# Low parts of w8 formed by VectorE differences instead of adding transfers

## The chip, the cores and the metric

The kernel runs on one core of a Trainium2 chip. The metric is the device time of one launch in microseconds; the median over several runs is compared. Five engines work side by side, each taking its own instructions in order: TensorE (PE; its weight loads are listed apart as PEld), VectorE (DVE), ScalarE (ACT), GpSimd (POOL) and SyncE (SP), which here only issues transfers. They wait for one another by semaphores. Transfers run on 16 DMA engines.

## What is computed

Two transformer layers on a sequence of 512 tokens with 1024 features, in float32. The first layer mixes four kinds of heads and ends with a gated FFN. The second one modulates its norms by a vector c, runs a state-space mixer beside windowed attention, and ends with the FFN in which the change lies:

```python
mod = (c_act @ w_mod[l] + b_mod[l])[:, None, :]
sh1, sc1, g1, sh2, sc2, g2 = jnp.split(mod, N_MOD, axis=-1)
...
h2 = _rms(x, norm2_w[l]) * (1 + sc2) + sh2
x = x + g2 * _conv_ffn(h2, w_up[l], conv_w[l], conv_b[l], w_down[l])

def _conv_ffn(h, w_up, conv_w, conv_b, w_down):
    up = h @ w_up
    up = <causal depthwise conv of width 3 over the tokens> + conv_b
    val, gate = jnp.split(up, 2, axis=-1)
    return (jax.nn.silu(gate) * val) @ w_down
```

w_up is 1024 x 5632 here (w8 in the kernel) and w_down 2816 x 1024 (w9).

## The kernel before, in words

**Split products.** Every matrix product is made of three products in the format fp32r, of which a value keeps only the upper part: hi = fp32r(w), lo = w - hi, and likewise for the activations; hi*hi + hi*lo + lo*hi is summed in PSUM (`mm3`, L451, called by `proj_f`, L457, and `proj_group`, L463). So each weight must be turned into a hi tile (`whi`) and a lo tile (`wlo`) before TensorE can use it.

**Weight pieces.** All weights stand in one list, `queue`, in the order in which they are used, cut into pieces of at most 128 x 1072 values (`cut`, L326). A w8 piece is 128 columns of w_up over all 8 k-tiles (512 KB), one group of 24 matmuls over 512 tokens; a w9 piece is 4 k-tiles by 256 columns, also 24 matmuls (the first four are half as large). `_Lazy.load` (L367) issues the transfer into a `raw` tile (two buffers, SP's queue), has ScalarE round it into `whi` (five buffers), and forms `wlo` (five buffers) in one of two ways:

```python
act(v(hi)[:, a:b], v(raw)[:, a:b], AF.Copy)                               # L374
if self.name in DMA_LO:
    act(lo[:, :m], raw[:, :m], AF.Copy, scale=-1.0)                       # L377
    nc.gpsimd.dma_start(v(lo), self.src[...], accum_op=ALU.add)           # L378
else:
    V.tensor_tensor(v(lo)[:, a:b], v(raw)[:, a:b], v(hi...), op=ALU.subtract)   # L381
```

The first way writes the negated rounded value and has a transfer issued by GpSimd add the weight from memory to it a second time. The second way is one VectorE instruction, which holds the raw buffer until it is done. Before, w6, w7 and w8 go the first way, all others the second.

**The second FFN** (`ffn`, L1254, called at L1738) walks over six chunks of hidden features: `up` makes for each hidden tile two groups (value and gate), `down` multiplies the chunk before by w9. Its groups take their PSUM banks in turn from three pools, tr (2 banks), sc (2) and acc (3). `hidden2` (L1723) evacuates a pair: for each half ScalarE writes `cf` from PSUM (L1717) and VectorE adds two shifted rows to it (L1719, 511 and 510 columns wide); then Silu (L1726), a product (L1727) and the split into `hd` (L507, L508). `down2` (L1733) adds a w9 product to x.

**Modulation rows.** The last eight rows of the modulation (g2, `modG`) are computed in the head of this FFN: `modulation` (L1069) is a generator that is advanced twice after each group of the FFN; each row is two transfers of 256 KB into `wm` (three buffers, SP's queue) and two VectorE reductions with the vector `cb` (L1082). Each is held back until the split of the latest hidden tile has been issued.

**Before the FFN** stands the norm (`norm_tail`, L1291): the six last tiles of x are made in two halves of tokens, squared by ScalarE (L1340), summed by VectorE (L1342), and normalised (L512 to L521); `modulated` (L1358) makes h2 from them, `hm` and `hl` on VectorE, `hl` on ScalarE. The first three w8 pieces are loaded during this time; a limit on the list keeps the others back until h2 is complete, after which `go_on` (L390) loads the next one. The first three groups run k-tile by k-tile as h2 comes (`start_ffn2`, L1690).

The order of instructions on each engine is set by the scheduler of the language from its own estimates, except on TensorE where parts are held in the order written.

Of the kernel before, what the change touches and what calls it, by code (L numbers as in the profile page):

```python
# [46 lines left out]
NW = 16  # L47
NHL = 5
SUM_E = "vector"
DMA_LO = ("w6", "w7", "w8")  # L50
LAG = 4
NRAW = 2
NW2 = 19
# [179 lines left out]
def build(tc, I, out, PV, PVN, CS, CSN, CS1, CSN1):  # L233
# [105 lines left out]
    class _Lazy:  # L339
# [27 lines left out]
        def load(self):  # L367
# [5 lines left out]
            for a, b in self.halves():  # L373
                act(v(hi)[:, a:b], v(raw)[:, a:b], AF.Copy)  # L374
            if self.name in DMA_LO:
                k0, k1, c0, c1 = self.cut
# [1390 lines left out]
```

## Time and profile before

| | |
|---|---|
| median of three runs | 1287.53 us (1284.62 to 1288.72) |
| the profiled execution | 1290.43 us |
| its span, first to last instruction | 1288.6 us |
| TensorE busy | 1230.1 us, 95% |
| VectorE busy | 836.3 us, 65% |
| ScalarE busy | 553.8 us, 43% |
| GpSimd busy | 312.1 us, 24% |
| moved by DMA | 192.95 MB, of them 40.61 MB on GpSimd's queue |
| w8 and w9 stage (second FFN) | from 901.89 us to the end |

Times in the rows are microseconds from the start of the span. "Idle before" a group is the time that its engine stood just before its instructions, and the name behind the arrow is what ended that wait. A granted clock of 1.00 is 2.4 GHz of TensorE, 0.50 is 1.2 GHz.

### The profile page before, as it was taken

The numbers are of one execution on the slowest core, as the hardware profiler recorded it, in microseconds if no ns is written. First come the engines' busy times: TensorE is split into PE (matmuls) and PEld (weight loads), VectorE is DVE, ScalarE is ACT, GpSimd is POOL, SyncE is SP. The second block draws the span as 40 slices with busy tenths as digits, with TensorE's granted clock in tenths as the row PEclk, the third lists the DMA queues.
The fourth block names the chain that finished last, engine by engine and source line by source line (L and its number), as shares of the span: only waits on it lengthen the run. The fifth ranks groups of instructions, "written<-read, shape, count | busy, mean of one in ns | idle before, by whom it ended". The sixth has DMA issues, their size and how long they took to land.

```text
span 1288.6 us, 17279 instructions
## 1 busy us (share of the span) xinstructions
PE 1230.1 (95%) x6269; PEld 993.0 (77%) x6269; DVE 836.3 (65%) x1622; ACT 553.8 (43%) x918; POOL 312.1 (24%) x399
## 2 busy tenths in 40 slices
PE   7899999999999999999999978889899999999998
PEld 6788765667887878888889877668777788888886
DVE  7668868677977967676667488756547343434362
ACT  6334465454332323232325235765655544444430
POOL 1000004113409283755201331032121211111200
PEclk9999999999999999999999887989899999999999
DMA  6431111126356665666547865457799989796921
GB/s 223 156 112 49 51 33 50 50 61 191 115 162 202 218 200 181 188 194 198 176 144 248 246 150 129 122 129 129 140 209 194 211 168 161 148 177 141 186 82 66
DMA packets 211156, 192.95 MB, mean 150 GB/s; under 512 B 13056, under 2 KB 173712, under 8 KB 211072
## 3 DMA queue, kind: packets, MB, share of 16 engines
q1 hardware_dynamic: 154528, 146.96, 37.8%
q0 software_dynamic: 51456, 40.61, 19.8%
q10 hardware_dynamic: 5088, 4.29, 1.0%
q8 instruction: 50, 0.82, 0.3%
q14 instruction: 34, 0.28, 0.1%
HBM read 178.22 MB, written 15.43 MB: 150 GB/s over the span
## 4 chain that ended last, share of the span: by engine, by line
PE 76%; DVE 9%; issue 5%; DMA 5%; ACT 4%; POOL 1%; SPq 0%; POOLq 0%; DVEq 0%; ACTq 0%
PE acc L261 51%; PE sc L261 12%; PE tr L261 8%; DMA raw<-in_w_dram 3%; PE po L261 2%; DMA wlo<-in_w_dram 2%; DVE wlo L381 1%; PE tr L886 1%; ACT whi L374 1%; DVE z L1478 1%; DVE z L1467 1%; PE tr L1616 1%; DVE z L1466 1%; POOL keep L929 0%; POOL wlo L378 0%
## 5 line engine op out<-in xcount | busy, mean ns | idle before, releaser
L261 PE MATMUL acc<-hl,whi 128*128 128x512 f32 (+1 forms) x1624 | 483.6, 381 | 10.3 <-ACT whi L374 6.1
L374 ACT ACTIVATE whi<-raw 128x1024 fp32r<-128x1024 f32 (+2 forms) x188 | 194.3, 1035 | 392.7 <-PE acc L261 231.4
L261 PEld LDWEIGHTS acc<-hl,whi 128*128 128x128 f32 x1624 | 295.3, 189 | 77.4 <-issue 9.2
L261 PE MATMUL acc<-hl,wlo 128*128 128x512 f32 (+1 forms) x812 | 308.5, 380 | 0.3 <-DMA wlo<-in_w_dram 0.3
L381 DVE TENSOR_TENSOR wlo<-raw,whi 128x1024 fp32r<-128x1024 f32 (+2 forms) x134 | 174.9, 1307 | 67.7 <-ACT whi L374 64.7
L261 PEld LDWEIGHTS acc<-hl,wlo 128*128 128x128 f32 x812 | 153.1, 189 | 31.6 <-issue 3.1
L378 POOL DMA_DIRECT2D wlo<-in_w_dram x54 | 72.0, 1334 | 326.7 <-ACT wlo L377 225.7
L261 PE MATMUL acc<-hd,whi 128*128 128x512 f32 (+1 forms) x472 | 143.1, 386 | 2.1 <-DVE x L1348 2.1
L261 PE MATMUL acc<-whi,hl 128*128 128x256 f32 (+1 forms) x544 | 110.3, 294 | 3.3 <-ACT whi L374 1.7
L261 PEld LDWEIGHTS acc<-hd,whi 128*128 128x128 f32 x472 | 87.0, 188 | 21.6 <-issue 3.1
L261 PEld LDWEIGHTS acc<-whi,hl 128*128 128x128 f32 x544 | 90.0, 197 | 8.8 <-ACT tok L248 3.0
L261 PE MATMUL acc<-hd,wlo 128*128 128x512 f32 (+1 forms) x236 | 91.0, 386 | 0.0
L1082 DVE CUSTOM_DVE_ANT_0 wm<-wm,cb 128x512 f32<-128x512 f32 x96 | 78.0, 844 | 14.3 <-DMA wm<-in_wmod_dram 14.2
L261 PE MATMUL acc<-wlo,hl 128*128 128x256 f32 (+1 forms) x272 | 79.4, 292 | 0.7 <-DVE wlo L381 0.7
L261 PE MATMUL tr<-hl,whi 128*128 128x512 f32 (+1 forms) x240 | 75.2, 397 | 0.0
L261 PE MATMUL sc<-hl,whi 128*128 128x512 f32 x208 | 65.0, 393 | 0.0
L377 ACT ACTIVATE wlo<-raw 128x1024 fp32r<-128x1024 f32 x54 | 56.5, 1045 | 4.8 <-DMA raw<-in_w_dram 2.8
L261 PE MATMUL tr<-hl,wlo 128*128 128x512 f32 (+1 forms) x120 | 48.1, 400 | 8.9 <-DMA wlo<-in_w_dram 8.9
L261 PEld LDWEIGHTS acc<-wlo,hl 128*128 128x128 f32 x272 | 53.8, 198 | 2.5 <-DVE wlo L381 1.0
L929 POOL TENSOR_SCALAR_AFFINE_SELECT keep<-keep 128x128 f32<-128x128 f32 x16 | 9.3, 594 | 185.8 <-ACT keep L923 185.0
L261 PEld LDWEIGHTS tr<-hl,whi 128*128 128x128 f32 x240 | 46.3, 196 | 10.2
L261 PEld LDWEIGHTS acc<-hd,wlo 128*128 128x128 f32 x236 | 44.4, 188 | 9.4
(427 smaller groups left out, 1945.6 us busy)
## 6 DMA issues: line engine op xcount, KB each, us to landing
raw<-in_w_dram SPq DMA_DIRECT2D x176, 512.0 KB, 4.4
wlo<-in_w_dram POOLq DMA_DIRECT2D x54, 512.0 KB, 7.8
wm<-in_wmod_dram SPq DMA_DIRECT2D x96, 256.0 KB, 4.1
xk<-in_xT_dram SPq DMA_DIRECT2D x16, 256.0 KB, 4.6
raw<-in_w_dram SPq DMA_DIRECT2D x10, 256.0 KB, 4.0
d_g<-s5g POOLq DMA_DIRECT2D x4, 576.0 KB, 4.0
gt<-d_g SPq DMA_DIRECT2D x4, 576.0 KB, 6.1
w1c<-in_w1k_dram SPq DMA_DIRECT2D x8, 256.0 KB, 6.1
```

What stands on the lines that cost most here:

```text
L261: nc.tensor.matmul(o, lhsT=l, rhs=r, start=start, stop=stop, **k)
L374: act(v(hi)[:, a:b], v(raw)[:, a:b], AF.Copy)
L377: act(lo[:, :m], raw[:, :m], AF.Copy, scale=-1.0)
L378: nc.gpsimd.dma_start(v(lo), self.src[:, k0:k1, c0:c1], accum_op=ALU.add)
L381: V.tensor_tensor(v(lo)[:, a:b], v(raw)[:, a:b], v(hi.bitcast(F32))[:, a:b], op=ALU.subtract)
L886: nc.tensor.transpose(tp[:, q * P:(q + 1) * P], pr[hh][:, j * P:(j + 1) * P], ident)
L929: G.affine_select(g[:, d], g[:, d], fill=1.0, **past)
L1082: V.tensor_tensor_reduce(wm, wm, cb[:, n * 512:(n + 1) * 512], 1.0, 0.0, ALU.mult, ALU.add, mh[:, n, j:j + 1])
L1466: V.scalar_tensor_tensor(dst[re], src[im], sign, t[im], op0=ALU.mult, op1=ALU.mult)
L1467: V.scalar_tensor_tensor(dst[im], src[re], -sign, t[re], op0=ALU.mult, op1=ALU.mult)
L1478: V.tensor_tensor_scan(z2[:, c], mag8[:, q * 8 + g:q * 8 + g + 1].to_broadcast([P, 64]), z[:, c], 0.0, ALU.mult, ALU.add)
L1616: nc.tensor.transpose(tp[:, m * P:(m + 1) * P], probs[n][:, hh, (j - j0) * P:(j - j0 + 1) * P], ident)
```

## The change

One name is taken out of a tuple; nothing else differs between the two files.

```diff
@@ -47,7 +47,7 @@
 NW = 16
 NHL = 5
 SUM_E = "vector"
-DMA_LO = ("w6", "w7", "w8")
+DMA_LO = ("w6", "w7")
 LAG = 4
 NRAW = 2
 NW2 = 19
```

With it the 44 pieces of w8 take the second way in `load`: L377 and L378 are not issued for them, L381 is. w6 and w7 keep the first way. The description of the change also speaks of evenly spaced modulation rows; their code is the same in both files. The scheduler sets some instructions in another order. Three places show it; a row is line, operation, out<-in and shape, and x2 stands for two such rows.

VectorE between the norm and the first evacuations of the second FFN: `hl` is the low part of h2, `cf` the conv rows of the first two groups.

```order
 L1362 SCALAR_TENSOR_TENSOR hm<-x_7_8176,a_3143,r_8191 128x256
 L1367 SCALAR_TENSOR_TENSOR hl<-hm,modT,hl 128x256 x2
+L381 TENSOR_TENSOR wlo<-raw,whi 128x1024 x2
 L1719 SCALAR_TENSOR_TENSOR cf<-acc,pv,cf 128x511 x2
 L1719 SCALAR_TENSOR_TENSOR cf<-acc,pv,cf 128x510 x2
 L1719 SCALAR_TENSOR_TENSOR cf<-acc,pv,cf 128x511
+L381 TENSOR_TENSOR wlo<-raw,whi 128x1024
+L1727 TENSOR_TENSOR cf<-cf 128x512
 L1719 SCALAR_TENSOR_TENSOR cf<-acc,pv,cf 128x510
-L1727 TENSOR_TENSOR cf<-cf 128x512
 L1719 SCALAR_TENSOR_TENSOR cf<-tr,pv,cf 128x511
```

The differences of the fourth and fifth piece come right behind h2, that of the sixth between the conv rows of the first groups.

ScalarE at the same place:

```order
 L519 ACTIVATE rsq<-r_8191 128x256
 L1366 ACTIVATE hl<-hm,modT 128x256 x9
-L374 ACTIVATE whi<-raw 128x1024
-L377 ACTIVATE wlo<-raw 128x1024
-L374 ACTIVATE whi<-raw 128x1024
-L377 ACTIVATE wlo<-raw 128x1024
+L374 ACTIVATE whi<-raw 128x1024 x2
 L1074 ACT_TABLE_LOAD
 L1074 ACTIVATE cb<-cb 128x1024
 L1717 ACTIVATE cf<-acc,pv 128x512 x3
```

The negated copies of the fourth and fifth piece are gone from between the two roundings.

VectorE in the norm, where the second w8 piece is made ready (`xa` and `x` are the sums of a tile of x, `sqsum` the sum of squares):

```order
 L1679 SCALAR_TENSOR_TENSOR xa<-acc,gm,r_a 128x512
 L1680 TENSOR_TENSOR x_1_7983<-x_1_7983,xa 128x512
+L381 TENSOR_TENSOR wlo<-raw,whi 128x1024
 L1679 SCALAR_TENSOR_TENSOR xa<-acc,gm,r_a 128x256
+L1342 TENSOR_TENSOR sqsum<-sqsum,sq 128x512
 L1680 TENSOR_TENSOR x_2_8011<-x_2_8011,xa 128x256
-L1342 TENSOR_TENSOR sqsum<-sqsum,sq 128x512
 L1679 SCALAR_TENSOR_TENSOR xa<-acc,gm,r_a 128x256
```

A difference stands between the tiles 1 and 2 of x; another stands earlier, ahead of the root for r_a, and a third between the second halves of tiles 3 and 4, just ahead of the root of this norm. On TensorE only the small products of the norm move by two or three matmuls. On GpSimd the 44 issues of L378 are missing. On SP the loads of raw and of modulation rows change places a few times.

## Rows read from the trace of the kernel before

**Rows 1.** The page: busy us (share of the span) and instructions of each engine
```profile
PE 1230.1 (95%) x6269; PEld 993.0 (77%) x6269; DVE 836.3 (65%) x1622; ACT 553.8 (43%) x918; POOL 312.1 (24%) x399
```
**Rows 2.** Busy time by stage: stretch, length, PE PEld DVE ACT POOL, clock, DMA, GB/s
```profile
400.00:690.00 290.00, 289.81 (x1343) 236.09 (x1342) 204.95 (x302) 89.16 (x117) 138.77 (x211) 1.00 0.60 187
...
925.00:930.00 5.00, 2.94 (x7) 2.42 (x8) 1.38 (x3) 1.17 (x3) 1.44 (x1) 0.50 1.32 223
...
915.00:985.00 70.00, 61.02 (x269) 49.56 (x269) 34.05 (x69) 37.38 (x48) 12.94 (x9) 0.93 1.03 208
985.00:1240.00 255.00, 254.05 (x1098) 205.90 (x1096) 111.62 (x147) 119.94 (x143) 45.99 (x32) 1.00 0.88 166
```
**Rows 3.** TensorE's waits after 905 us: in total, times, longest
```profile
PE tr L261 <- DMA wlo<-in_w_dram: 8.9, 2, 6.4
PE sc L261 <- DMA wlo<-in_w_dram: 0.6, 1, 0.6
PE acc L261 <- DMA wlo<-in_w_dram: 0.3, 1, 0.3
```
**Rows 4.** TensorE in order of time: start, length, instruction [idle before <-releaser]
```profile
901.89 0.97 PE L261 MATMUL acc<-hl,whi 128*128 128x256 f32 x4 [2.75 <-ACT hl L1366]
...
920.00 0.63 PE L261 MATMUL tr<-hl,whi 128*128 128x512 f32 x2
927.06 0.77 PE L261 MATMUL tr<-hl,wlo 128*128 128x512 f32 x1 [6.43 <-DMA wlo<-in_w_dram]
...
934.11 0.63 PE L261 MATMUL sc<-hl,whi 128*128 128x512 f32 x2
...
945.18 0.63 PE L261 MATMUL tr<-hl,whi 128*128 128x512 f32 x2
```
**Rows 5.** The chain that ended last, in order of time: start, length, what
```profile
955.14 5.53 PE sc L261 x24
960.67 5.61 PE acc L261 x24
```
**Rows 6.** ScalarE in order of time, 911 to 931 us
```profile
914.69 1.04 ACT L374 ACTIVATE whi<-raw 128x1024 fp32r<-128x1024 f32 x1
915.64 1.04 ACT L377 ACTIVATE wlo<-raw 128x1024 fp32r<-128x1024 f32 x1
...
923.11 1.06 ACT L374 ACTIVATE whi<-raw 128x1024 fp32r<-128x1024 f32 x1 [0.16 <-DMA raw<-in_w_dram]
```
**Rows 7.** GpSimd in order of time, 880 to 950 us
```profile
916.97 1.44 POOL L378 DMA_DIRECT2D wlo<-in_w_dram  x1 [19.73 <-ACT wlo L377]
```
**Rows 8.** Transfers issued 905 to 960 us: count, size, median us to landing
```profile
raw<-in_w_dram SPq DMA_DIRECT2D x7, 512.0 KB, 10.8
wlo<-in_w_dram POOLq DMA_DIRECT2D x7, 512.0 KB, 12.6
```
**Rows 9.** Transfers issued 1000 to 1240 us
```profile
raw<-in_w_dram SPq DMA_DIRECT2D x44, 512.0 KB, 4.3
wlo<-in_w_dram POOLq DMA_DIRECT2D x29, 512.0 KB, 7.6
```
**Rows 10.** VectorE by form, 400 to 690 us: busy, mean ns | idle before, releasers
```profile
L381 DVE TENSOR_TENSOR wlo<-raw,whi 128x1024 fp32r<-128x1024 f32 x52 | 78.1, 1502 | 10.0 <-ACT whi L374 9.9
```
**Rows 11.** VectorE by form, 960 to 1289 us
```profile
L381 DVE TENSOR_TENSOR wlo<-raw,whi 128x1024 fp32r<-128x1024 f32 x20 | 24.3, 1221 | 23.0 <-ACT whi L374 22.7
...
L1719 DVE SCALAR_TENSOR_TENSOR cf<-tr,pv,cf 128x510 f32<-128x510 f32 x13 | 9.7, 748 | 0.4
```
**Rows 12.** VectorE in order of time, in the norm before the second FFN
```profile
892.17 0.48 DVE L1679 SCALAR_TENSOR_TENSOR xa<-acc,gm,r_a 128x256 f32<-128x256 f32 x1 [1.36 <-PE acc L261]
...
895.86 0.42 DVE L1342 TENSOR_TENSOR sqsum<-sqsum,sq 128x256 f32<-128x256 f32 x1 [0.98 <-ACT sq L1340]
...
897.12 0.42 DVE L520 SCALAR_TENSOR_TENSOR rsq<-sc,rsq 128x256 f32<-128x256 f32 x1 [0.44 <-ACT rsq L519]
```
**Rows 13.** ScalarE in order of time, in the same stretch
```profile
894.47 1.04 ACT L377 ACTIVATE wlo<-raw 128x1024 fp32r<-128x1024 f32 x1
```

## The prediction

> **What bounds the kernel now.** I read the page's busy times first: TensorE is busy 1230.1 us of 1288.6, VectorE 836.3, ScalarE 553.8 [rows 1]. A gain can only come out of the 58 us in which TensorE stands, or out of matmuls at a low clock. The change touches only the last stage, the second FFN, so the next view is the busy time by stage [rows 2]. The reader is to see three things there. The first FFN, 400 to 690 us, already forms its low parts by VectorE differences and has TensorE busy 289.81 of 290 us. The second FFN, which forms those of w8 by adding transfers, has 254.05 of 255 us from 985 on. Only its head is torn: 61.02 of 70 us between 915 and 985, and the granted clock is 0.50 between 925 and 930, the lower of its two levels (1.2 GHz).
>
> Who makes TensorE stand there is told by its waits after 905 us: nothing but wlo landing late, 8.9 us in two waits, 0.6 in one, 0.3 in one [rows 3]. So the wall that the change takes down is the only one in this stage; behind it stands TensorE itself.
>
> To price a wait I use pieces. A w8 piece (128 columns, 8 k-tiles) feeds 24 matmuls, and an undisturbed one takes 5.53 us [rows 5]. I number the pieces in the order of use: 1 to 3 are worked together with the norm, 4 begins at 920.00, 5 at 934.11, 7 at 945.18 [rows 4], 8 at 955.14, 9 at 960.67 [rows 5]. Piece 4 therefore takes 14.11 us, 8.58 too many: 6.43 of standing, the rest matmuls at the low clock. Pieces 5 and 6 take 11.07, as they should. Piece 7 takes 9.96, 4.43 too many.
>
> **What the change removes.** For each of the 44 pieces of w8 it removes a ScalarE copy of 1.04 us [rows 6] and a transfer of 512 KB issued by GpSimd (1.44 us [rows 7], 7.6 us to land in the steady part [rows 9]). Neither engine bounds this stage, so the busy time saved is worth nothing by itself. What counts is the chain of piece 4: whi is copied at 914.69, the negated copy made at 915.64 [rows 6], the transfer issued at 916.97 [rows 7], and TensorE goes on with its wlo at 927.06, having waited 6.43 us [rows 4]. In the head, 905 to 960 us, the transfers are far slower than elsewhere: raw 10.8 us and wlo 12.6 [rows 8], against 4.3 and 7.6 later [rows 9]. Half of the w8 bytes that are moved there go.
>
> **What it adds.** 44 VectorE differences. The same instruction on w9 pieces in this very stage takes 1.221 us [rows 11], so 53.7 us in all; in the first FFN it takes 1.502 [rows 10]. Cover: from 985 on VectorE works 111.62 of 255 us [rows 2]; 31 of the 44 fall there, 38 us, which makes some 150 of 255, less than the 204.95 of 290 with which the first FFN loses nothing. In the head, 915 to 985, VectorE works 34.05 us; ten differences more make 46.3 in what would then be 57 us, 81%. If that cover were gone, each piece would cost its 1.22 us.
>
> On the two prices: rows 10 show 1.502 us in the stage where GpSimd is busy 138.77 of 290 us, rows 11 show 1.221 where it has 45.99 of 255, all of it issues of the transfers that go [rows 2, 7]. The Trainium skill, page "SBUF — State Buffer", section "Who interferes with whom", says that a VectorE instruction with two SBUF inputs contends with a GpSimd instruction that reads SBUF. By that rule the new differences keep the lower price, as nothing is left on GpSimd in this stage; with a GpSimd that computed there, the rule would add 44 times 0.28, 12 us of VectorE time, and the second rival below would weigh more.
>
> **Does the new chain arrive in time?** I walk it by the order of the changed program. ScalarE copies whi of piece 4 at 914.69 for 1.04 us [rows 6]; the difference stands right behind the last half of h2 on VectorE, so wlo is there at about 917.0, and TensorE wants it at 920.5. Piece 5: whi to 916.7, difference to 918.2, wanted at 925.5. Piece 6: its raw buffer is free at 917.0; with the landing of before it was copied at 923.1 [rows 6], and its difference stands behind five conv instructions and ends near 926, wanted at 931.1. Piece 7: buffer free at 918.2; its difference stands behind two modulation halves and conv work that waits for piece 4's matmuls (925.5), so it ends near 931, wanted at 936.6. Piece 8 near 933.4, wanted at 942.2. The lead is never under 3.5 us and grows after that, since five wlo buffers let the loads run four pieces ahead. What queues behind a waiting difference on VectorE are conv evacuations, for which a PSUM bank waits only six products later (33 us), and modulation rows, which nobody needs before the first w9 product. SP's queue loses nothing: the loads of raw only change places with modulation rows.
>
> **The norm in front.** Three differences now stand in VectorE's work before 901.89 [rows 4]. Nothing like that is in the trace, so I bound it. The second comes while VectorE runs behind TensorE, and costs its 1.22 us there; but by 892.17 VectorE had caught up and waited 1.36 us for TensorE [rows 12]. The third stands just before the norm's root. VectorE idles there 0.98 us for a square and 0.44 for the root [rows 12], and ScalarE does that square only after the negated copy of 894.47 [rows 13]; the copy goes (1.04 us) and the difference comes (1.22). So the bounds are +1.2 (a difference wholly on the chain) and -1.0 (the copy gone, the difference in idle time); I take 0, because the idle rows nearly equal the new work.
>
> **The sum.** 8.58 + 4.43 + 0.6 + 0.3 = 13.9 us. Steady part 0, norm 0, the last w9 products unchanged. The profiled execution took 1290.43 us (span 1288.6, 1.8 around it), so it would take 1276.5. It lies 2.9 above the median of the three runs, 1287.53; on that scale the result is **1273.6 us**.
>
> **Rivals.** First, only one of the two holes closes. cb and three modulation halves, 1.25 MB, are issued at the same time as raw of pieces 6 and 7. For it speaks the raw landing of 10.8 us in this stretch [rows 8]: raw of piece 6 would land at 927.8 and its difference end near 932, almost 1 us late; raw of piece 8, which waits for that buffer, would land near 942 and its difference end near 945, about 3 late, which with the low clock is the 4.43 of the second hole. Time 1287.5 - 9.5 = 1278.0. Against it: half of that crowd is the adding transfers.
>
> Second, the hole only changes its name: VectorE takes its work strictly in order, differences queue behind conv instructions that themselves wait for TensorE, and the head stays nearly as torn. With a gain under 3.9 us the time is 1284 to 1291. It needs some 10 us of lateness against leads of 3.5 us and more. For it stands the 81%; at the first FFN's price per difference [rows 10] ten would take 2.8 us more, 49 of 57, still under.
>
> Third, slower: the two raw buffers become the bound. Now ScalarE alone frees a raw buffer of w8; then it is free only when VectorE has come to its difference. A buffer's round is landing L, copy 1.04, difference 1.22 and the queueing q on VectorE; two buffers must give a piece each 5.54 us, so it decides from L + q = 8.8 us. With L of 4.3 [rows 9], q may be 4.5. Should q be 7.2, a round is 13.8 and a piece takes 6.9; the 31 later pieces lose 1.35 each, 42 us less the 13.9 gained: about 1316. For it: conv_ff puts four conv instructions of 0.75 us per pair of pieces [rows 11] in front of a difference, more than the first FFN has. Against it: the first FFN has the same two buffers and the same differences, and TensorE does not wait [rows 2].
>
> That the change doesn't do what it says is excluded for w8: in the order 44 rows leave ScalarE and GpSimd and 44 come on VectorE. The even spacing that its name speaks of is not in the diff; modulation rows only slip behind differences, and their cost is in the 81%.
>
> **How the numbers follow.** The forecast gets 0.71, the first rival 0.17, the second 0.07, the third 0.05. Faster by over 0.3% (below 1283.7; about what a measurement of this kernel can tell from no change) is the forecast with the first rival, 0.88; the same 0.07; slower 0.05. The range: the fastest run of before, 1284.62, less 13.9 is 1270.7, with a part of the norm's -1.0 it is 1270; above, the first rival with the norm's +1.2 and the spread of some 2 us between runs gives 1281.
>
> **What would show it.** Right: after 905 us TensorE waits for no wlo, the granted clock is 1.00 from 905 on, piece 9 begins near 947.7, differences take 1.22 us, VectorE has near 150 of 255 us in the steady part. First rival: one wait of TensorE between 931 and 950, ended by VectorE's L381. Second: VectorE waits for whi ahead of conv rows and TensorE stands several times. Third: TensorE waits in every piece, and raw is copied the moment it lands. Wrong in another way would be a start of the first w8 product later than 901.89: then the norm's bound was too kind.

## The result, and the profile after

The changed kernel takes 1272.53 us (median of four runs, 1269.89 to 1276.42) against 1286.22 us of the kernel before on the same chip: a ratio of 0.987, 95% interval 0.984 to 0.990. That is 13.7 us by the medians. The forecast was 13.9 us less and 1273.6 us, range 1270 to 1281. The profiled execution took 1273.53 us, its span is 1271.8.

First the page of the kernel after: busy us of each engine, as in [rows 1], and the line of GpSimd's transfer queue (packets, MB, share of 16 engines).

```profile
PE 1220.6 (96%) x6269; PEld 986.8 (78%) x6269; DVE 888.4 (70%) x1666; ACT 512.6 (40%) x874; POOL 251.8 (20%) x355
...
q0 software_dynamic: 5696, 17.54, 5.4%
```

44 instructions more on VectorE, 44 fewer on ScalarE and on GpSimd, and that queue moves 17.54 MB where it moved 40.61. Next the waits of TensorE from 860 us to the end (who waited for what, total us, times, longest), which answers to [rows 3]:

```profile
PE acc L261 <- ACT hl L1366: 2.0, 1, 2.0
PE sc L261 <- DVE sqsum L1342: 0.3, 1, 0.3
```

Both belong to the norm. No wait for wlo is left. The busy time by stage of the kernel after (stretch, length, PE, PEld, DVE, ACT, POOL, granted clock, DMA share, GB/s), to be held against [rows 2]:

```profile
905.00:920.00 15.00, 15.00 (x122) 14.66 (x121) 12.15 (x26) 10.40 (x16) 0.00 (x0) 1.00 0.48 142
...
925.00:930.00 5.00, 5.00 (x23) 4.08 (x22) 5.00 (x11) 2.75 (x4) 0.00 (x0) 1.00 0.51 141
930.00:940.00 10.00, 10.00 (x45) 8.13 (x44) 9.16 (x17) 4.00 (x6) 0.00 (x0) 1.00 0.66 213
940.00:960.00 20.00, 20.00 (x88) 16.23 (x87) 17.24 (x34) 9.00 (x13) 0.00 (x0) 1.00 0.70 207
915.00:972.00 57.00, 57.00 (x262) 46.90 (x261) 46.04 (x83) 28.71 (x37) 0.00 (x0) 1.00 0.58 173
972.00:1226.00 254.00, 254.00 (x1099) 206.29 (x1098) 146.70 (x175) 89.83 (x111) 0.00 (x0) 1.00 0.34 100
```

TensorE is full in every row at clock 1.00. VectorE is nearly full between 925 and 940 us (14.16 of 15) and is busy for 146.70 of 254 us later.

Where the time went is read from landmarks on TensorE: the start of the products with tot_s (ahead of w7, so ahead of anything that the change touches), of those with tot_a (just ahead of the last w7 products and the norm), of piece 4 and of piece 9. Three lines of the kernel before, then four of the kernel after (start us, us, instruction):

```profile
844.82 1.52 PE L261 MATMUL sc<-tot_s,cst 128*128 128x512 f32 x2
...
874.55 1.02 PE L261 MATMUL sc<-tot_a,cst 128*128 128x512 f32 x2
...
960.50 0.62 PE L261 MATMUL acc<-hl,whi 128*128 128x512 f32 x2
```

```profile
843.04 1.61 PE L261 MATMUL sc<-tot_s,cst 128*128 128x512 f32 x2
...
872.82 1.02 PE L261 MATMUL sc<-tot_a,cst 128*128 128x512 f32 x2
...
918.08 0.62 PE L261 MATMUL tr<-hl,whi 128*128 128x512 f32 x2
...
945.79 0.62 PE L261 MATMUL acc<-hl,whi 128*128 128x512 f32 x2
```

Piece 4 of before began at 920.00 [rows 4]; its piece 9 begins at 960.50 here, where the chain of [rows 5] has 960.67, so the head is 40.50 below and not 40.67. So, of the 16.8 us between the two spans: 1.78 lie ahead of tot_s, where both kernels run the same instructions in the same order; tot_s to piece 4 took 75.18 and takes 75.04 (0.14); piece 4 to piece 9, "the head" below, 40.50 and 27.71 (12.79); the rest 328.10 and 326.01 (2.09). From tot_s on the change is worth 15.0 us.

### The profile page after: what moved, and what is told of

Read it like the earlier page. It is cut to its first block, busy times and chain, and to the rows that moved or that the text cites. A ratio compares the mean times of both kernels' runs of the same rounds, so it can differ in the third digit from the quotient of the medians.

```text
span 1271.8 us, 17124 instructions
## 1 busy us (share of the span) xinstructions
PE 1220.6 (96%) x6269; PEld 986.8 (78%) x6269; DVE 888.4 (70%) x1666; ACT 512.6 (40%) x874; POOL 251.8 (20%) x355
## 3 DMA queue, kind: packets, MB, share of 16 engines
q0 software_dynamic: 5696, 17.54, 5.4%
## 4 chain that ended last, share of the span: by engine, by line
PE 81%; DVE 8%; issue 3%; ACT 3%; DMA 3%; POOL 1%; SPq 0%; POOLq 0%; ACTq 0%; DVEq 0%
PE acc L261 53%; PE sc L261 13%; PE tr L261 10%; PE po L261 2%; DMA raw<-in_w_dram 2%; DVE wlo L381 1%; PE tr L886 1%; ACT whi L374 1%; PE tr L1616 1%; DVE z L1478 1%; DVE z L1467 1%; DVE z L1466 1%; POOL keep L929 0%; DMA ua<-d_u 0%; DVE keep L930 0%
## 5 line engine op out<-in xcount | busy, mean ns | idle before, releaser
L381 DVE TENSOR_TENSOR wlo<-raw,whi 128x1024 fp32r<-128x1024 f32 (+2 forms) x178 | 226.1, 1272 | 110.2 <-ACT whi L374 106.0
L261 PEld LDWEIGHTS sc<-hl,whi 128*128 128x128 f32 x208 | 39.1, 188 | 9.0
L1348 DVE TENSOR_TENSOR x<-x,acc 128x512 f32<-128x512 f32 (+1 forms) x49 | 31.6, 655 | 19.2 <-PE acc L261 19.2
```

The source lines that it names most:

```text
L261: nc.tensor.matmul(o, lhsT=l, rhs=r, start=start, stop=stop, **k)
L381: V.tensor_tensor(v(lo)[:, a:b], v(raw)[:, a:b], v(hi.bitcast(F32))[:, a:b], op=ALU.subtract)
L1348: done[0] = V.tensor_tensor(x[k][:, cs], x[k][:, cs], ps[:, cs], op=ALU.add)
```

## The experiments

Every kernel below was also profiled once, and the same landmarks are read from its trace. "From tot_s" is the end of the span less the start of tot_s; "front" is from tot_s to piece 4, and its three parts are from tot_s to tot_a, from there to the first w8 product, and from there to piece 4; all in us. What each kernel is follows below; the six that are made from the kernel before ran once.

| kernel | span | tot_s starts | front | its three parts | head | rest | from tot_s |
|---|---|---|---|---|---|---|---|
| before | 1288.6 | 844.82 | 75.2 | 29.73 + 27.34 + 18.11 | 40.50 | 328.1 | 443.8 |
| after | 1271.8 | 843.04 | 75.0 | 29.78 + 27.15 + 18.11 | 27.71 | 326.0 | 428.8 |
| after, once more | 1272.0 | 843.13 | 75.2 | 29.92 + 27.16 + 18.11 | 27.72 | 326.0 | 428.9 |
| differences for pieces 4 to 12 | 1278.8 | 846.52 | 77.8 | 30.93 + 27.35 + 19.47 | 27.72 | 326.8 | 432.3 |
| for piece 4 alone | 1275.5 | 839.76 | 75.0 | 29.58 + 27.34 + 18.11 | 31.81 | 328.9 | 435.7 |
| for pieces 13 to 44 | 1287.9 | 845.77 | 77.6 | 30.81 + 27.35 + 19.41 | 38.16 | 326.4 | 442.1 |
| for pieces 1 to 3 | 1286.6 | 842.05 | 77.2 | 30.64 + 27.13 + 19.46 | 38.73 | 328.6 | 444.6 |
| before, fourth piece loaded early | 1285.7 | 845.84 | 79.6 | 30.79 + 28.14 + 20.66 | 30.04 | 330.2 | 439.9 |
| before, modulation rows moved | 1292.0 | 852.41 | 76.9 | 29.64 + 27.60 + 19.69 | 34.85 | 327.8 | 439.6 |
| after, differences twice | 1277.6 | 841.50 | 77.5 | 30.75 + 28.67 + 18.11 | 30.38 | 328.2 | 436.1 |
| after, a maximum of wlo added | 1276.2 | 842.00 | 77.8 | 29.47 + 28.67 + 19.65 | 28.20 | 328.2 | 434.2 |

In the last two the scheduler sets the first two matmuls of a piece among those of the piece before; there piece 9 is taken where piece 8 ends.

The first part of the front holds no work on w8 by TensorE. It takes 29.5 to 29.9 us in six of these kernels and 30.6 to 30.9 in five, where the granted clock of its first 10 us is 0.82 to 0.84 instead of 0.93 to 0.97. The last part takes 18.11 us, or over a microsecond more where the clock falls (last section). The middle part is the norm.

**Differences for a part of w8.** Four kernels are the kernel before in which only some of the 44 pieces take the second way:

```diff
-            if self.name in DMA_LO:
+            n8 = [p_ for p_ in queue if p_.name == "w8"].index(self) + 1 if self.name == "w8" else 0
+            if self.name in DMA_LO and not 4 <= n8 <= 12:
```

Pieces 4 to 12:

> The kernel before, with only pieces 4 to 12 of w8 by VectorE differences (pieces 1 to 3 and 13 to 44 by adding transfers). Measure: from the first matmul of piece 4 to the first of piece 9, 40.67 us before and 27.71 after the change (27.7 is five pieces without a stall). My theory, that the whole gain lies in the two holes of the head: 27.7, no wait for wlo before piece 13; the small waits further on (0.33 and 0.62 us before) stay, so piece 9 to the end takes about 324. Rival, that the relief of VectorE's partners in the steady part or in the norm gives the gain: the head stays above 33.

Measured: 1280.47 us, with 1289.34 for the kernel before beside it. The waits of TensorE after 905 us:

```profile
PE acc L261 <- ACT hl L1367: 2.7, 1, 2.7
PE acc L261 <- DMA wlo<-in_w_dram: 0.5, 1, 0.5
```

The head takes 27.72 us, the same as with all 44. Nine pieces carry the whole gain of the head; the 0.5 us wait stands at piece 13, where the adding transfers begin again. The front is 2.6 longer, and that hides part of the gain in the total: 1.2 of it lie between tot_s and tot_a and 1.4 right behind the norm, both at a low granted clock; the norm itself takes what it took.

The same edit with `13 <= n8 <= 44`:

> The kernel before, with only pieces 13 to 44 of w8 by VectorE differences. My theory: the head keeps both holes, about 40.7 us from piece 4 to piece 9 (39 to 43), and from piece 9 to the end the small waits go, 322.1 instead of 323.9. Rival, that the steady part gives a good share: the end comes over 4 us earlier after piece 9, or the head shrinks below 36.

Measured: 1289.71 us. The waits after 905 us:

```profile
PE tr L261 <- DMA wlo<-in_w_dram: 6.4, 2, 4.5
PE sc L261 <- DMA wlo<-in_w_dram: 0.6, 1, 0.6
```

Both holes are there, head 38.16 us, a little under the 39 to 43 expected: piece 4 takes 13.09, and pieces 7 and 8 take 7.68 and 6.34. From piece 9 on it takes 326.4, 0.4 more than after; piece 11, still by an adding transfer, takes 5.88. So the 32 late pieces are worth most of the small waits and no more.

With `1 <= n8 <= 3`:

> The kernel before, with only pieces 1 to 3 of w8 by VectorE differences, those that stand in the norm. Measure: from the first matmul of the last w7 column groups (a block of 24 matmuls into acc just ahead of the norm) to the first matmul of piece 4: 44.43 us before, 44.40 after. My theory: 44.4 within 0.6, and the head keeps about 40.7. Rival, that three differences in the norm cost VectorE's full 1.22 us each: 45.6 to 48. Rival, that the negated copies that go speed the norm up: 43.4.

Measured: 1288.27 us. The waits after 905 us:

```profile
PE tr L261 <- DMA wlo<-in_w_dram: 8.2, 3, 6.1
PE acc L261 <- DMA wlo<-in_w_dram: 1.0, 1, 1.0
PE sc L261 <- DMA wlo<-in_w_dram: 0.6, 1, 0.6
```

The holes stay, head 38.73. From tot_a to piece 4 it takes 46.59 us, against 45.45 before and 45.26 after. That is 1.1 more than before, so by the expectation's own measure, which starts a microsecond later, some 45.6: outside my 0.6 and at the lower edge of the first rival's range. But the time is not in the norm. From tot_a to the first w8 product it takes 27.13 us, against 27.34 before and 27.15 after, and 27.34 or 27.35 in the kernels with differences for pieces 4 to 12, 13 to 44 or piece 4 alone, which keep the adding transfers in the norm. What is longer is the stretch behind the norm, by 1.35 us, at the low clock. So the three differences take about 0.2 us off the norm, and neither rival is right.

With `4 <= n8 <= 4`, piece 4 alone:

> The kernel before, where the fourth w8 piece alone is formed by a VectorE difference. By the prediction's sum the first hole, 8.58 us, is piece 4's alone and goes; the second, 4.43 us at piece 7, stays: head 40.67 - 8.6 = 32.1 us. If the two holes are one lateness of the queue of adding transfers that is only met at piece 4 first, the hole moves to piece 5 or 6 and the head stays above 36 us.

Measured: 1277.28 us. The waits after 905 us:

```profile
PE tr L261 <- DMA wlo<-in_w_dram: 1.6, 2, 1.1
PE acc L261 <- ACT wlo L378: 1.5, 1, 1.5
PE sc L261 <- ACT hd L508: 1.5, 1, 1.5
PE sc L261 <- DMA wlo<-in_w_dram: 0.8, 1, 0.8
```

(The one put down to hd stands ahead of a product with wlo of piece 5.) The head is 31.81, forecast 32.1. One difference takes the first hole out, 8.7 us. What is left of the second is 4.1, but not at piece 7 in one lump: pieces 5, 7 and 8 take 7.24, 6.96 and 6.53 instead of 5.54. So the second hole is not piece 7's own; it is the transfers' lateness, and where it stands depends on the pieces in front. The span is 13.1 us shorter than before, but this run was 5.1 us earlier at tot_s; from tot_s the gain is 8.0.

In the kernel before, the first hole had its part in it. Two of ScalarE's instructions there, an evacuation of piece 4 and the negated copy of piece 7:

```profile
934.30 0.78 ACT L1717 ACTIVATE cf<-tr,pv 128x512 f32<-128x512 f32 x1 [3.78 <-PE tr L261]
935.50 1.05 ACT L377 ACTIVATE wlo<-raw 128x1024 fp32r<-128x1024 f32 x1
```

whi of piece 7 was copied at 929.47, but the negated copy had to wait in ScalarE's order behind an evacuation that stood 3.78 us for the held-up products of piece 4. Its transfer was issued at 936.98 and had landed at 948.11.

**The first hole without any difference.** The kernel before with its limit on the list one piece later:

```diff
-    norm_tail((bp, ("w", NW2)), tot, r4, start_ffn2, wpieces["w8", 0][1], TAIL=TAIL2, NPOS=NPOS2)(product, w_out2)
+    norm_tail((bp, ("w", NW2)), tot, r4, start_ffn2, wpieces["w8", 1][1], TAIL=TAIL2, NPOS=NPOS2)(product, w_out2)
```

> The kernel before, with adding transfers for all of w8, but the limit on the list is set one piece later: the fourth w8 piece too is loaded during the norm, and only the fifth waits for h2. If the first hole is the late start of piece 4's chain (landing, two copies, an adding transfer that ended 6.43 us too late [rows 4]), it goes, and the head from piece 4 to piece 9, 40.67 us before, shrinks to some 32 to 34; the second hole stays, and may come earlier. If the first hole comes from crowded transfers and not from the start, whichever piece is loaded first after the norm is late by the same amount and the head stays within 2 us of 40.67; then the hole stands at piece 5.

Measured: 1287.54 us. Its waits after 905 us of more than a microsecond:

```profile
PE acc L261 <- ACT hl L1366: 3.5, 1, 3.5
PE acc L261 <- DMA wlo<-in_w_dram: 3.0, 2, 1.8
PE tr L261 <- DMA wlo<-in_w_dram: 1.8, 2, 1.1
```

Its busy time just behind the norm:

```profile
904.00:912.00 8.00, 7.23 (x34) 6.78 (x35) 8.00 (x22) 5.17 (x13) 0.00 (x0) 0.59 0.83 141
```

The hole at piece 4 is gone and none takes its place at piece 5: head 30.04, better than forecast. So the first hole was the late start of one chain. The head is that short because nearly half of the second hole now stands behind its end: pieces 6, 7, 9 and 10 take 6.96, 6.46, 6.12 and 6.91. From piece 4 to the start of piece 11 it takes 43.07 us, where the kernel before takes 51.65 and the one after 38.86: 8.58 are gone, the size of the first hole, and 4.2 are left. With the further piece's copies and transfer in the norm the front takes 79.6 us instead of 75.2: 0.8 more in the norm and 2.55 behind it, where the clock is 0.59; the other 1.1 lie between tot_s and tot_a, at a low clock too. From tot_s the gain is 3.9.

**What the modulation rows do to the holes.** The kernel before with the last eight rows made in the first FFN:

```diff
-MOD1 = 40
-MOD_RATE = 0.0275
+MOD1 = 48
+MOD_RATE = 0.0325
...
+    modG = modT[:, 40:48]
...
-    last8 = modulation(fp, MOD1, 48, modG)
+    last8 = iter(())
```

> The kernel before with adding transfers, but the last eight modulation rows are made in the first FFN with the others, so cb and 16 transfers of 256 KB are gone from the head of the second FFN. My theory has two causes in the head: the chain of piece 4 starts too late for an adding transfer whatever the crowd (whi 914.7, issue 917.0, at best 7.6 us to land: 924.6 against 920.5, so a standing of about 4 us and 1.5 us of slow matmuls stay), and the crowd makes the rest. So the head takes 32 to 34.5 us, with the second hole gone. Rival, all is the crowd: 28 to 29. Rival, the crowd is nothing: 40 or more. The first FFN loses under 1 us by it.

Measured: 1293.80 us. The waits after 905 us:

```profile
PE tr L261 <- DMA wlo<-in_w_dram: 5.1, 2, 4.5
PE acc L261 <- ACT hl L1366: 2.7, 1, 2.7
PE acc L261 <- DMA wlo<-in_w_dram: 1.2, 1, 1.2
```

The head is 34.85, just above the 32 to 34.5 expected. Three kernels have the rows and form piece 4 and those behind it by adding transfers loaded after the norm: before, pieces 13 to 44, and pieces 1 to 3. Their heads take 40.50, 38.16 and 38.73 us, so it is 3.3 to 5.65 us shorter without the rows, of the 10.4 to 12.8 that are lost there. Of this, 1.8 to 3.4 are the second hole, which is nearly gone: pieces 7 and 8 take 11.88 us together, against 15.32, 14.02 and 13.71. The rest is at piece 4. Its wait is 4.54 instead of 6.43, but that this is the rows' doing is not shown: with the rows in place it is 4.55 and 6.06 in the other two kernels. From the issue of piece 4's transfer to the first product with its wlo it takes 9.65 us here, and 10.09 [rows 4, 7], 8.35 and 9.91 in the three. In the first FFN and behind it the rows cost more than they give: tot_s starts 7.6 us later than before, and 5.9 later than in any other kernel of the table, with new waits of TensorE there, where I had expected under 1 us.

**How much cover VectorE has left.** The changed kernel with each difference of w8 made twice:

```diff
-                    V.tensor_tensor(v(lo)[:, a:b], v(raw)[:, a:b], v(hi.bitcast(F32))[:, a:b], op=ALU.subtract)
+                    for _ in range(2 if self.name == "w8" else 1):
+                        V.tensor_tensor(v(lo)[:, a:b], v(raw)[:, a:b], v(hi.bitcast(F32))[:, a:b], op=ALU.subtract)
```

It ran beside the changed kernel once more:

> The changed kernel once more, beside the three that follow on the same chip, so that they can be compared with it. Its ratio to the kernel before was 0.987 in the first comparison; 0.985 to 0.989 is expected here.

> The changed kernel with every difference of w8 made twice, 44 further instructions of 1.22 us on VectorE (53.7 us in all), the second one writing the same values again. My theory says that VectorE's spare time covers the steady part: from 972 to 1226 us it is busy 146.7 of 254 us and would have some 180 to 190, less than the 204.95 of 290 of the first FFN [rows 2] gives by share, 71%. In the head it is busy 17 of each 20 us between 940 and 960; the modulation rows that stand there wait for nobody, so they slip; I expect at most 3 us there and in the norm, 0 to 3 us over the changed kernel in all. The third rival (two raw buffers become the bound, since a buffer is held until both differences are done) says that every piece is late: at 1 us a piece some 30 us or more over the changed kernel, with a wait of TensorE in each piece.

Measured: 1272.0 us for the changed kernel (1270.65 to 1274.33; ratio to before 0.986, 0.982 to 0.991) and 1280.2 (1279.46 to 1283.74; 0.994, 0.991 to 0.996) for the double one. 8.2 us, where I expected 0 to 3 and the third rival 30 or more: neither. Waits of TensorE in the double kernel from 868 us:

```profile
PE acc L261 <- ACT hl L1367: 3.1, 1, 3.1
PE tr L261 <- ACT whi L374: 1.5, 1, 1.5
PE acc L261 <- DVE wlo L382: 1.0, 1, 1.0
PE sc L261 <- ACT whi L374: 0.7, 1, 0.7
```

Two stretches of it, in the columns of above:

```profile
925.00:945.00 20.00, 18.62 (x78) 14.25 (x78) 17.25 (x31) 8.85 (x13) 0.00 (x0) 1.00 0.44 134
972.00:1226.00 254.00, 252.52 (x1092) 205.03 (x1091) 182.79 (x211) 91.83 (x114) 0.00 (x0) 1.00 0.35 103
```

From tot_s it loses 7.2: 0.8 between tot_s and tot_a, at a low clock, 1.5 in the norm, 2.7 in the head, 2.2 behind. The last row is the point on which my expectation was right: 36 us more VectorE work in the steady part cost TensorE 1.5 us. The rest is norm and the stretch up to some 970 us, where there was hardly any cover left. The waits for whi are waits for raw, and raw waits for its buffer (SP stood 44.8 us for differences in its issues of raw between 915 and 1000 us, 39.8 in the changed kernel): the third rival's mechanism, at three places and not in every piece.

To tell the buffer from VectorE's time, the next kernel has a second instruction of the same size that doesn't hold raw:

```diff
                     V.tensor_tensor(v(lo)[:, a:b], v(raw)[:, a:b], v(hi.bitcast(F32))[:, a:b], op=ALU.subtract)
+                    if self.name == "w8":
+                        V.tensor_tensor(v(lo)[:, a:b], v(lo)[:, a:b], v(lo)[:, a:b], op=ALU.max)
```

> The changed kernel with one further VectorE instruction of the same size per w8 piece, as in the kernel with every difference made twice, but this one takes the maximum of wlo with itself and so doesn't hold the raw buffer. The doubled differences cost 5.6 us of span over the changed kernel (1277.6 against 1272.0), 2.7 of them between piece 4 and piece 9, where whi waited for raw. If the raw buffers' round sets that, this kernel has no wait for whi in the head and loses 0 to 3 us against the changed kernel (what remains is the norm and VectorE's order). If VectorE's own time sets it, it loses the same 5 to 8 us, with waits for wlo or for conv rows in place of those for whi.

Measured: 1281.19 us (1276.42 to 1284.93 over ten runs; 0.994, 0.992 to 0.996): no better than the double one. The profiled execution, 1277.96, is one of its faster ones. TensorE's waits from 868 us:

```profile
PE acc L261 <- ACT hl L1368: 3.1, 1, 3.1
PE tr L261 <- ACT whi L374: 1.3, 1, 1.3
PE tr L261 <- DVE wlo L383: 0.8, 1, 0.8
```

The same two stretches:

```profile
925.00:945.00 20.00, 20.00 (x89) 16.22 (x88) 18.99 (x32) 7.84 (x11) 0.00 (x0) 1.00 0.51 157
972.00:1226.00 254.00, 252.66 (x1092) 204.87 (x1091) 183.20 (x209) 91.37 (x113) 0.00 (x0) 1.00 0.35 103
```

The group of the new instruction from 900 to 1226 us (count, busy us, mean ns, idle before):

```profile
L383 DVE TENSOR_TENSOR wlo<-wlo 128x1024 fp32r<-128x1024 f32 x41 | 49.8, 1218 | 0.4
```

In the head the buffer does matter: 28.20 against 30.38, and 925 to 945 us is full. The rest loses 2.2, as in the double kernel, again with a wait for whi. The norm loses 1.5, also as in the double kernel: both take 28.67 us from tot_a to the first w8 product, the changed kernel 27.16. Behind it 1.5 are lost by the low clock. So of the double kernel's 7.2 us, by one profile of each, 2.2 are the held buffer, 0.8 the clock ahead of tot_a, and the other 4.2 are VectorE's time in the order in which it comes. My expectation of at most 3 is refuted by the medians. Why the medians of the two kernels agree although the profiled spans differ by 1.4 stays open; the ten runs spread over 8.5 us, and thirteen of the kernel before beside them over 8.6.

**The other weights.** The changed kernel without any adding transfer, and with w6 alone keeping it:

```diff
-DMA_LO = ("w6", "w7")
+DMA_LO = ()
```

> The changed kernel with no adding transfer at all: w6 and w7, the weights of the stage between the two FFNs, are formed by VectorE differences too. That stage has VectorE busier than the FFN (some 28 to 33 of 40 us between 760 and 840 us) and TensorE waits for it there, so nothing is certain: if transfers are late there, up to 2 us are gained (one wait of 2.1 us for raw stands in that stage); if VectorE is what ends there, each of the differences that falls on the chain costs 1.2 us, and with some 24 pieces up to 10 us are lost. I expect between -2 and +6 us against the changed kernel, and take +2.

> As the one before it, but w7 alone is formed by VectorE differences and w6 keeps the adding transfers. w6 is used in the fuller part of the stage, w7 behind it and ahead of the norm. I expect between -2 and +3 us against the changed kernel, and take 0.

Measured: 1271.37 us (0.986, 0.982 to 0.990) and 1273.76 us (0.987, 0.983 to 0.992), against 1272.0 for the changed kernel beside them: no difference that shows. I had counted some 24 pieces; the two weights have ten. In the first of the two kernels TensorE's wait of 2.5 us for raw between 690 and 870 us is gone, and one for a difference stands in its place:

```profile
PE acc L261 <- DVE wlo L381: 2.4, 1, 2.4
```

Other waits there grow or shrink by up to 2.7 us. No version here is shown to beat the changed kernel.

## Where the prediction held and where it failed, point by point

**The step that failed.** The mechanism came true: the waits for wlo are gone, and nothing took their place. The term of the sum that was wrong is that of the small waits, 0.6 + 0.3 us, which I priced at the idle time that the profile lists. Piece 9 to the end gave 2.09 us, more than twice as much. So the traces show 15.0 us from tot_s on, where the sum has 13.9. That the medians differ by 13.7 is luck to that extent: beside the later experiments they differ by 15.4 (1287.36 and 1272.0), and what lies ahead of tot_s differs by up to 6.8 us between kernels that are the same there. A second step was wrong without harm to the sum: the two holes were priced as two separate delays, and they are not.

**The bound.** TensorE behind two holes and nothing else: held. After 905 us no wait for wlo is left, and the clock is 1.00 in each row from 905 on.

**The two holes, 8.58 + 4.43 = 13.0.** The head gave 12.79. That the first is the chain of piece 4 is shown by two runs (piece 4 alone by a difference: 8.7; its chain started earlier: 8.58 up to piece 11). The second I had put down as piece 7's own. Without the first hole it stood at pieces 5, 7 and 8 in one run, and at pieces 6, 7, 9 and 10 in the other, with 4.1 and 4.2 us in all: the transfers are late, and in the kernel before the first hole also held up piece 7's negated copy. The size was right, the place was not.

**The small waits, 0.6 + 0.3.** Of the 2.09 us, 1.8 are at pieces 11, 13 and 15, which take 0.37, 0.58 and 0.87 longer than after, in three short stands. The profile listed two of them, 0.33 and 0.62; the third is 0.11 of "issue" in the chain. In the run with pieces 4 to 12 one wait listed at 0.5 cost 0.8 of 326.0. A short wait costs here about a quarter of a microsecond more than its listed idle time; where in the matmuls behind it that lies was not followed.

**The new chain in time.** Held. VectorE's differences in the head of the kernel after:

```profile
913.86 2.36 DVE L381 TENSOR_TENSOR wlo<-raw,whi 128x1024 fp32r<-128x1024 f32 x2 [0.46 <-ACT whi L374]
...
921.69 1.22 DVE L381 TENSOR_TENSOR wlo<-raw,whi 128x1024 fp32r<-128x1024 f32 x1
...
928.76 1.22 DVE L381 TENSOR_TENSOR wlo<-raw,whi 128x1024 fp32r<-128x1024 f32 x1
931.16 1.22 DVE L381 TENSOR_TENSOR wlo<-raw,whi 128x1024 fp32r<-128x1024 f32 x1
```

Piece 4 is ready at 915.0, 5 at 916.2, 6 at 922.9, 7 at 930.0, 8 at 932.4; I had 917.0, 918.2, 926, 931 and 933.4. Of that, 1.92 us are only that piece 4 begins earlier, at 918.08 and not at 920.00; with that taken off, 4 and 5 came as walked, 6 came 1.2 earlier, 7 and 8 came 0.9 later. Against the starts of the pieces, 918.08 and then 5.54 each, the leads are 3.0, 7.4, 6.3, 4.7 and 7.9 us; to piece 4's first product with wlo, as the walk counted, it is the 3.5. raw landed in 4.8 us there, not in 10.8 [rows 8]: half of the crowd was the adding transfers, as the argument against the first rival had it.

```profile
raw<-in_w_dram SPq DMA_DIRECT2D x7, 512.0 KB, 4.8
```

**The cover.** I wrote 81% for the head and some 150 of 255 us later. Both held: 46.04 of 57 us from 915 to 972, which is 81%, and 146.70 of 254, which the double kernel showed to be real cover. But the 81% is an average: in the 30 us from 930 on VectorE has 26.4, 88%. That was enough, but the double kernel lost 2.7 in the head.

**The price.** A difference takes 1.22 us, in the head above and in the steady part (count, busy us, mean ns):

```profile
L381 DVE TENSOR_TENSOR wlo<-raw,whi 128x1024 fp32r<-128x1024 f32 x48 | 58.7, 1223 | 63.2 <-ACT whi L374 61.9
```

GpSimd has 0.00 us in that stretch. By the rule of the Trainium skill ("SBUF — State Buffer", "Who interferes with whom") the low price was to be expected with GpSimd idle, and this trace agrees. With the issues of L378 on GpSimd it was 1.221 too [rows 11]; no run here shows that the 1.502 of [rows 10] is due to GpSimd's work.

**The norm.** Zero, between -1.0 and +1.2: it gave -0.14 from tot_s to the start of piece 4, and -0.19 from tot_a to the first w8 product. The exchange that I reckoned can be seen, VectorE's difference and ScalarE's square that no longer waits for a negated copy:

```profile
893.32 1.23 DVE L381 TENSOR_TENSOR wlo<-raw,whi 128x1024 fp32r<-128x1024 f32 x1
...
893.33 0.42 ACT L1340 ACTIVATE sq<-x 128x256 f32<-128x256 f32 x1
```

The two kernels with a second instruction show that this idle time is used up: three more in the norm delay the first w8 product by 1.5 us in each, counted from tot_a.

**The rivals.** The first (one hole stays) did not come, though its cause is real: without the modulation rows the head is 3.3 to 5.65 us shorter. The second did not come: VectorE's order held every lead. The third did not come, but it is the nearest: 1.22 us more per piece is enough for TensorE to wait for raw.

## What to carry to other kernels

When a stage is torn at its start only, price the pieces at the start and look for the chain that begins late; nine of 44 pieces carried 12.8 of the 15.0 us here, and one of them 8.7 of these. A busy share that is low over a stage says nothing of its first 40 us, where norm, evacuations and weight preparation meet: add the new work to the fullest slice. A short wait can cost more than its listed idle time: compare the lengths of the pieces. Compare traces from a landmark in front of the change, since the part ahead of it can differ by more than the effect that is looked for.

## What was unexpected in the hardware

- **The part ahead of the change moves by itself.** Kernels whose instructions stand in the same order up to tot_s (all of the table but the one with moved modulation rows) start it between 839.76 and 846.52 us, 6.8 us apart. In the stretch from 770 to 810 us the granted clock was 0.73 in the kernel before and 0.84 in the kernel with piece 4 alone. Single totals of this kernel can't tell apart effects of less than that.
- **The clock behind the norm.** From the first w8 product to piece 4 it takes 18.11 us in seven of the kernels (before, after and piece 4 alone among them), and 19.4 to 20.7 in the six others. There the granted clock fell, here in the kernel with pieces 4 to 12:

```profile
904.00:908.00 4.00, 3.20 (x11) 2.85 (x12) 4.00 (x11) 1.75 (x4) 0.00 (x0) 0.60 0.43 56
```

  TensorE had stood 2.73 us just before. But it had stood 2.71 in the kernel with piece 4 alone, and the clock stayed at 1.00; and it fell after 2.03 in the one with pieces 1 to 3. In the kernel before it had stood 2.75 us, with no fall either [rows 4]. The length of the stand alone doesn't tell it.
- **What the adding transfers of w8 cost the DMA engines.** GpSimd's queue of the kernel before, on its page (packets, MB, share of 16 engines):

```profile
q0 software_dynamic: 51456, 40.61, 19.8%
```

  Against the line of after it lost 23.07 MB in 45,760 packets (504 bytes each), and 255 - 69 = 186 us of all 16 engines: 8.1 us per MB. What stays on that queue, the ten adding transfers of w6 and w7 among it, has 3,079 bytes a packet and takes 3.9 us per MB. The small packets and the adding are not told apart by this; together they come with twice the price of a byte.
